# Reordering the scan's inserts between weight products in a Mamba-2 layer: decay product first, state product last, transposes ahead of the B-C products

## The chip, the cores and the metric

The kernel runs on one core of a Trainium2 chip. The metric is device time in microseconds, the median over runs. The engines named below are TensorE (PE, with its weight loads shown apart as PEld), VectorE (DVE), ScalarE (ACT), GpSimd (POOL) and SyncE (SP, whose queue issues most of the DMAs).

## The reference

One layer of a Mamba-2 mixer with a residual and two RMS norms, on 512 tokens of 2048 channels, in float32. Cut to what matters:

```python
hn = rmsnorm(x, ln_g)
proj = hn @ w_in                              # 2048 -> z 4096, x 4096, B 8*128, C 8*128, dt 64
xbc = silu(causal_depthwise_conv(xbc))        # 4 taps
dt = softplus(dt + dt_bias); a = -exp(a_log)
# scan over chunks, 64 heads of 64 channels, 8 groups of 8 heads that share B and C (128 states)
cs = cumsum(dt * a)
y_diag = einsum(C B^T, exp(cs_l - cs_s) masked to s <= l, x * dt)
y_off  = einsum(C, state, exp(cs))
state  = state * exp(cs_last) + einsum(B, exp(cs_last - cs), x * dt)
y = (y_diag + y_off + D * x) * silu(z)
out = rmsnorm(x + rmsnorm(y) @ w_out)
```

## The kernel before

The 512 tokens stand in the free dimension, channels in the partitions. The input projection is cut into 80 tiles of 128 channels. Each float32 weight tile is loaded, cast by ACT to a high part (`hi`, line 87) and its remainder is taken by DVE (`lo`, line 88); a product is then three matmuls (`hi` by `xh`, `hi` by `xl`, `lo` by `xh`).

A head pair is a "unit": 32 units `u`, four to a group `g`. A unit needs an x tile and a z tile, a group a B and a C tile. The first eight tiles (B0 C0 x0 z0 x1 z1 B1 C1) are multiplied plainly, 16 steps each. From step 128 on, the other tiles go two by two through `pair(n, prev)`, which multiplies a two by two block of weights with seven products (R11, T1, T2, R22, R21, T3, T4) over sums and differences of blocks instead of eight. A pair is 28 steps long, a step is two `k` of a product, so six matmuls; the seventh product of a pair (`last`) runs inside the next pair. There are 36 pairs, 32 of x and z, with a pair of B and C ahead of the third unit of each group. Then comes the output projection, from step 1136, with products of the same two kinds.

Between the weight products stand the small matmuls of the scan, called inserts here. They are put at steps: `add(step, f, *a)` appends a function to the list `ev[step]`, and `run(step)`, which the product loops call at the start of each step, calls that list in the order in which it was filled. So two inserts at one step run in the order of their `add` calls. The inserts of a unit are:

- `u_load` issues three DMAs on SP's queue: `csb` (the cumulated decay of two heads, spread over the partitions, one buffer) and `ecs`, in two parts.
- `u_decay` makes the decay matrix `m` (one buffer): 12 small ACT instructions, one large ACT exponential, and one DVE product with `cbm`.
- `u_xt` transposes `xs` by four matmuls into the bank `tr` (line 473); DVE makes `xd` and `xw` from it (lines 476 and 479).
- `u_state` makes the state product of `Bt` and `xw` in the bank `yo` (line 488), which ACT and DVE split into `stsh` and `stsl` (lines 403 and 404, in an `urgent` block).
- `u_yd` is the product of `xd` and `m` in the bank `yd` (lines 502 and 506), in two halves of 64 columns of the array; DVE then makes `y` from it (line 509).
- `u_yo` multiplies `Cs` and the split state (lines 518 to 520); DVE ends `y` from it (lines 521 to 523) and SP stores it (line 524).

For units 2 to 31 their steps count from the unit's own pair: 28, 42, 56, 65, 65 and 71, so `u_state` and `u_yd` share a step. Units 0 and 1 have steps of their own (`ramp`), where those two lie apart. The inserts of a group are `g_bt` (two transposes of B, for 6 of the groups at the step where unit 4g-2 has `u_state` and `u_yd`) and `g_cb` (the products of B and C in the banks `yd` and `yo`, lines 433 and 434, then `cbm`; for groups 1 to 7 at the step where unit 4g-1 has `u_xt` and unit 4g has `u_load`). Weight loads, splits and sums of a pair (`q_events`) are added after all of these, so at a shared step they follow the inserts.

TensorE, SP and GpSimd run in program order (`MANUAL`). DVE and ACT are ordered by a planner, which walks through the instructions with modelled times; instructions in an `urgent` block have priority.

Of the kernel before, what the change touches and what calls it, by code (L numbers as in the profile page):

```python
# [27 lines left out]
NU = G * UPG  # L28
# [6 lines left out]
def mamba_layer(ctx: ExitStack, tc: tile.TileContext, d: dict, out: bass.AP):  # L35
# [83 lines left out]
    at = {s: i * KT for i, s in enumerate(plain)}  # L119
# [584 lines left out]
    def add(step, f, *a):  # L704
        ev.setdefault(step, []).append((f, a))

    for g in range(1, G):
        add(at["B", g] + (30 if ("B", g) in plain else 93), g_bt, g)
        for i in range(2):
            add(at["x", 4 * g] + 28, g_cb, g, i)  # L710
    ramp = [[66, 71, 63, 75, 87, 92], [56, 65, 50, 68, 86, 92]]
    for u in range(NU):
        w = ramp[u] if u < len(ramp) else [28, 42, 56, 65, 65, 71]
        for o, f in zip(w, (u_load, u_decay, u_xt, u_state, u_yd, u_yo)):
            add(at["x", u] + o, f, u)
    for n in range(len(quads)):
        q_events(n, NPL * KT + n * QS, n == len(quads) - 1, 0 if n else 14, lone=not n)
    for i in range(4):
# [393 lines left out]
```

## Time and profile before

| what | value |
|---|---|
| median of 3 runs | 1294.51 us (1292.67 to 1301.33) |
| the profiled execution's own time | 1295.7 us |
| its span, first to last instruction | 1294.0 us |
| mean granted TensorE clock | 0.991 |
| PE busy, share of the span | 97% |
| DVE busy | 84% |
| ACT busy | 64% |
| DMA, mean rate | 175 GB/s |

The profile tells of one execution. A timeline row has the start, the time from it to the end of the row's last instruction, engine, line, what is written from what, the shape, how many instructions were merged, and in brackets the idle time before it and what ended that. A row of the waits has the engine and tile that waited, whom it waited for, the total in us, how often, and the longest. Matmuls are pipelined: a row of one matmul says 0.28, but the next starts some 0.11 us after it, so costs on TensorE are read from start to start.

### The profile page before, as it was taken

Reading aid. Unit: us, or ns where it says so; the run is one execution under the profiler, and the core shown is the slowest. Engines: PE = TensorE matmul, PEld = TensorE weight load, DVE = VectorE, ACT = ScalarE, POOL = GpSimd, SP = SyncE. Lnnn points to the kernel's source line nnn. Section 1 sums busy time; section 2 is a strip of 40 time slices with the busy share of each in tenths; the row PEclk is TensorE's granted clock in tenths of the full one; section 3 lists DMA queues with packets and bytes.
Section 4 is the critical chain, followed back from the end, with each engine's and each line's share of the span. In section 5 each row is a group of like instructions: output and inputs, shape, how many; then the busy total and the mean of one; then the engine's idle time right before and its main releaser. Section 6 shows DMA issues by size and latency. Waiting matters only on the chain.

```text
span 1294.0 us, 24519 instructions
## 1 busy us (share of the span) xinstructions
PE 1252.1 (97%) x9932; PEld 1192.9 (92%) x9932; DVE 1084.3 (84%) x1449; ACT 826.6 (64%) x1357; POOL 77.5 (6%) x99
## 2 busy tenths in 40 slices
PE   8989899999999999999999999999999899999997
PEld 8989899999999999999999999999988899899885
DVE  5796988988989898998889899889857877887865
ACT  7667667677666757767685867778666445434433
POOL 0000001010000101010100001000000000000000
PEclk9989999999999999999999999999999999999999
DMA  9546657585676667667667677766637576647612
GB/s 356 179 141 172 162 161 174 143 215 142 192 197 174 159 169 183 164 176 199 162 161 195 151 188 171 212 155 154 185 105 258 146 199 199 197 119 229 183 57 98
DMA packets 70194, 225.90 MB, mean 175 GB/s; under 512 B 8384, under 2 KB 12800, under 8 KB 69952
## 3 DMA queue, kind: packets, MB, share of 16 engines
q1 hardware_dynamic: 56688, 176.34, 40.2%
q0 software_dynamic: 12672, 46.14, 22.1%
q8 instruction: 78, 1.28, 0.4%
q10 hardware_dynamic: 720, 1.84, 0.4%
q14 instruction: 36, 0.29, 0.1%
HBM read 211.52 MB, written 12.78 MB: 173 GB/s over the span
## 4 chain that ended last, share of the span: by engine, by line
PE 74%; DVE 11%; DMA 7%; issue 4%; ACT 3%; SPq 0%; POOL 0%; DVEq 0%; ACTq 0%; POOLq 0%
PE S L637 7%; PE S L635 7%; PE S L636 7%; PE mm L635 5%; PE mm L636 4%; PE R L635 4%; PE mm L637 4%; PE R L636 4%; PE R L637 4%; DVE lo L88 3%; PE mm L929 3%; PE mm L931 3%; PE mm L930 3%; PE yd L502 2%; PE mm L867 2%
## 5 line engine op out<-in xcount | busy, mean ns | idle before, releaser
L87 ACT CAST hi<-ra 128x1024 fp32r<-128x1024 f32 x150 | 154.7, 1046 | 159.5 <-DVE ra L604 72.9
L88 DVE TENSOR_TENSOR lo<-ra,hi 128x1024 fp32r<-128x1024 f32 x150 | 181.3, 1221 | 24.2 <-ACT hi L87 24.1
L635 PE MATMUL mm<-xh,hi 128*128 128x256 f32 x576 | 163.6, 284 | 0.0
L637 PE MATMUL mm<-xh,lo 128*128 128x256 f32 x576 | 160.6, 279 | 0.6 <-DVE lo L88 0.6
L636 PE MATMUL mm<-xl,hi 128*128 128x256 f32 x576 | 160.4, 278 | 0.0
L637 PE MATMUL R<-s,lo 128*128 128x256 f32 x576 | 160.3, 278 | 0.1
L635 PE MATMUL R<-s,hi 128*128 128x256 f32 x576 | 160.2, 278 | 0.0
L636 PE MATMUL R<-s,hi 128*128 128x256 f32 x576 | 160.2, 278 | 0.0
L88 DVE TENSOR_TENSOR lo<-rc,hi 128x1024 fp32r<-128x1024 f32 x94 | 114.9, 1223 | 28.5 <-ACT hi L87 28.1
L87 ACT CAST hi<-rc 128x1024 fp32r<-128x1024 f32 x94 | 98.4, 1047 | 50.8 <-issue 29.1
L604 DVE TENSOR_TENSOR ra<-ra,rc 128x1024 f32<-128x1024 f32 x88 | 107.7, 1224 | 13.3 <-DMA rc<-in_wi 11.8
L635 PEld LDWEIGHTS mm<-xh,hi 128*128 128x128 f32 x576 | 108.1, 188 | 5.2 <-issue 5.0
L637 PEld LDWEIGHTS mm<-xh,lo 128*128 128x128 f32 x576 | 109.2, 190 | 0.8 <-DVE lo L88 0.8
L637 PEld LDWEIGHTS R<-s,lo 128*128 128x128 f32 x576 | 109.1, 189 | 0.3 <-DVE lo L88 0.3
L635 PEld LDWEIGHTS R<-s,hi 128*128 128x128 f32 x576 | 108.2, 188 | 0.0
L636 PEld LDWEIGHTS mm<-xl,hi 128*128 128x128 f32 x576 | 108.2, 188 | 0.0
L636 PEld LDWEIGHTS R<-s,hi 128*128 128x128 f32 x576 | 108.1, 188 | 0.0
L637 PE MATMUL S<-xh,lo 128*128 128x256 f32 x288 | 83.5, 290 | 5.6 <-DVE lo L88 5.6
L635 PE MATMUL S<-xh,h1h 128*128 128x256 f32 x288 | 83.4, 290 | 1.0 <-DVE xr L398 1.0
L635 PE MATMUL S<-xh,hi 128*128 128x256 f32 x288 | 81.3, 282 | 2.2 <-ACT xh L577 1.3
L636 PE MATMUL S<-xl,hi 128*128 128x256 f32 x288 | 81.2, 282 | 0.7 <-DVE xl L578 0.7
L636 PE MATMUL S<-xl,h1h 128*128 128x256 f32 x288 | 80.8, 280 | 0.0
(452 smaller groups left out, 3940.8 us busy)
## 6 DMA issues: line engine op xcount, KB each, us to landing
rc<-in_wi SPq DMA_DIRECT2D x76, 512.0 KB, 5.9
ra<-in_wi SPq DMA_DIRECT2D x42, 512.0 KB, 6.2
rb<-in_wi SPq DMA_DIRECT2D x40, 512.0 KB, 6.9
ra<-in_wi POOLq DMA_DIRECT2D x36, 512.0 KB, 6.3
rb<-in_wi POOLq DMA_DIRECT2D x36, 512.0 KB, 5.9
csb<-cscr SPq DMA_DIRECT2D x32, 512.0 KB, 8.0
ra<-in_wo SPq DMA_DIRECT2D x26, 512.0 KB, 5.4
yscr<-xs SPq DMA_DIRECT2D x32, 256.0 KB, 2.6
```

The source lines that it names most:

```text
L87: S.copy(out=hi, in_=raw)
L88: V.tensor_tensor(out=lo, in0=raw, in1=hi, op=ALU.subtract)
L502: T.matmul(pyd[r, i, :], x[:, 2 * i, hh, :], m[:, i, hh::4, :], start=i == 0, stop=False, skip_group_check=True)
L604: V.tensor_tensor(out=raw, in0=raw, in1=qs[n][other], op=ALU.add)
L635: T.matmul(ps, hi[:, k, :], ah, start=first and k == 0, stop=False, skip_group_check=True)
L636: T.matmul(ps, hi[:, k, :], al, start=False, stop=False, skip_group_check=True)
L637: T.matmul(ps, lo[:, k, :], ah, start=False, stop=k == KH - 1, skip_group_check=True)
L867: T.matmul(ps[:, t, :], yh[:, k, tt], hi[:, k, :], start=st, stop=False, skip_group_check=True)
L929: T.matmul(ps, yh, hi, start=first and k == 0, stop=False)
L930: T.matmul(ps, yh, lo, start=False, stop=False)
L931: T.matmul(ps, yl, hi, start=False, stop=last and k == 1)
```

## The change

The six functions of a unit are no longer added unit by unit behind all of the group's. They are added in four rounds: load, decay and xt of all units; then yd of all; then the group's `g_bt` and `g_cb`; then state and yo. The steps themselves stay. So at a shared step the order changes:

- at 30 steps (units 2 to 31): `u_state`, `u_yd` becomes `u_yd`, `u_state`; at 6 of them `g_bt`, `u_state`, `u_yd` becomes `u_yd`, `g_bt`, `u_state`;
- at 7 steps: `g_cb` twice, `u_xt`, `u_load` becomes `u_xt`, `u_load`, `g_cb` twice;
- at step 156: `u_yo` of unit 1, `u_load` of unit 2 becomes `u_load`, `u_yo`.

No instruction is added or removed.

```diff
+    ramp = [[66, 71, 63, 75, 87, 92], [56, 65, 50, 68, 86, 92]]
+    steps = [ramp[u] if u < len(ramp) else [28, 42, 56, 65, 65, 71] for u in range(NU)]
+
+    def add_units(*kinds):
+        for u in range(NU):
+            for i, f in kinds:
+                add(at["x", u] + steps[u][i], f, u)
+
+    add_units((0, u_load), (1, u_decay), (2, u_xt))
+    add_units((4, u_yd))
     for g in range(1, G):
         add(at["B", g] + (30 if ("B", g) in plain else 93), g_bt, g)
         for i in range(2):
             add(at["x", 4 * g] + 28, g_cb, g, i)
-    ramp = [[66, 71, 63, 75, 87, 92], [56, 65, 50, 68, 86, 92]]
-    for u in range(NU):
-        w = ramp[u] if u < len(ramp) else [28, 42, 56, 65, 65, 71]
-        for o, f in zip(w, (u_load, u_decay, u_xt, u_state, u_yd, u_yo)):
-            add(at["x", u] + o, f, u)
+    add_units((3, u_state), (5, u_yo))
```

## The prediction

> **What bounds the kernel now.** I read the page first, then busy time by stage, then TensorE's waits.
>
> ```profile
> PE 1252.1 (97%) x9932; PEld 1192.9 (92%) x9932; DVE 1084.3 (84%) x1449; ACT 826.6 (64%) x1357; POOL 77.5 (6%) x99
> ```
> ```profile
> 170.00:970.00 800.00, 794.64 (x6752) 768.50 (x6751) 705.03 (x907) 568.10 (x974) 57.53 (x67) 1.00 0.66 171
> 970.00:1294.00 324.00, 304.60 (x1985) 276.40 (x1983) 247.88 (x342) 143.02 (x197) 13.73 (x16) 0.99 0.56 169
> ```
> The second fence is the table by stage: start and end in us, length, then busy us of PE, PEld, DVE, ACT and POOL. The reader is to see that TensorE is the bound of the stage where the changed inserts lie (170 to 970 us): it is busy 794.6 of 800 us, so 5.4 us of idle time is all that better order could win there by ending waits. DVE is second with 705 of 800, and has some 95 us of air; ACT has 232. The rest of TensorE's idle time (19.4 of 324 us) lies in the output projection, which the change does not touch.
>
> Which waits those are, for 60 to 1000 us:
> ```profile
> PE S L637 <- DVE lo L88: 5.6, 9, 1.5
> ...
> PE tr L473 <- DVE win L366: 0.6, 1, 0.6
> ```
> The list has ten rows, and of the operations that the change moves only one is in it: a transpose (L473), once, in the ramp. No row has L488 (state), L502 or L506 (decay product), or L433 and L434 (B-C). So **no insert that changes places waits for anything today**; the waits of the stage are of weight products for a split (L637 for `lo`), which stand elsewhere in the pair. An order that lets an insert wait less cannot win on TensorE. What is left is the cost of changing from one kind of matmul to another, and what DVE and ACT do with other arrival times.
>
> **The change on TensorE: state and decay product.** The timeline at unit 11, today's order, with two rows of its `u_yo`:
> ```profile
> 422.54 0.28 PE L635 MATMUL mm<-xh,hi 128*128 128x256 f32 x1
> ...
> 422.77 0.28 PE L637 MATMUL mm<-xh,lo 128*128 128x256 f32 x1
> 422.88 0.60 PE L488 MATMUL yo<-xw,bt 128*128 128x128 f32 x4
> 423.42 0.65 PE L502 MATMUL yd<-m,xd 128*64 128x256 f32 x4
> ...
> 424.55 0.39 PE L506 MATMUL yd<-m,xd 128*64 128x128 f32 x4
> 424.87 0.39 PE L635 MATMUL mm<-xh,hi 128*128 128x256 f32 x1
> 425.09 0.28 PE L636 MATMUL mm<-xl,hi 128*128 128x256 f32 x1
> ...
> 429.08 0.28 PE L518 MATMUL yo<-csth,stsh 128*128 128x256 f32 x1
> ...
> 429.31 0.28 PE L520 MATMUL yo<-csth,stsl 128*128 128x256 f32 x1
> ```
> Products follow each other by (422.77 - 422.54) / 2 = 0.115 us. From 422.77 to 425.09 are 2.32 us with two products in them, so the two inserts cost 2.32 - 0.23 = **2.09 us**. The dear places are the change to the 64-column form and the way back: the state's four matmuls take 0.54 instead of about 0.44, the step out of the decay product is 0.21 (424.55 to 424.87 less a pair's 0.11), and the second product behind it comes after 0.22 instead of 0.115.
>
> The new order needs three transitions that this row doesn't have: product to decay product, decay product to state, state to product. The ramp has the first and the last, because units 0 and 1 run the two apart:
> ```profile
> 103.46 0.61 PE L488 MATMUL yo<-xw,bt 128*128 128x128 f32 x4
> 103.82 0.48 PE L198 MATMUL mm<-xh,hi 128*128 128x256 f32 x2
> 104.14 0.40 PE L198 MATMUL mm<-xl,hi 128*128 128x256 f32 x2
> 104.38 0.40 PE L198 MATMUL mm<-xh,lo 128*128 128x256 f32 x2
> ```
> ```profile
> 112.48 0.39 PE L198 MATMUL S<-xh,lo 128*128 128x256 f32 x2
> 112.80 0.65 PE L502 MATMUL yd<-m,xd 128*64 128x256 f32 x4
> ...
> 114.25 0.50 PE L198 MATMUL S<-xh,hi 128*128 128x256 f32 x2
> 114.59 0.40 PE L198 MATMUL S<-xl,hi 128*128 128x256 f32 x2
> ```
> Two products take 0.24 here. The state product alone: 104.14 - 103.46 = 0.68, less 0.24, is 0.44. The decay product alone: 114.59 - 112.80 = 1.79, less 0.24, is 1.55, and its entry is 0.32 instead of 0.24, so 1.63. Together 2.07, against 2.09 in one insert: **the costs add up, and no neighbour makes either cheaper**. Only decay product to state is not shown. Leaving the decay product costs a product 0.21 and then 0.105 of a late second start. Upper bound: the state pays both and the first products behind it pay the same again (0.2 more, by the nearest row, 424.55), 32 x 0.2 = +6.4 us. Lower bound: the state hides the second part, 32 x -0.105 = -3.4 us. (I count 32 for 30 units.) I take 0, since a state matmul and a product are both 128*128 forms and both show a start-to-start time of 0.11 behind their own kind.
>
> The late second start is 0.105 us long. The Trainium skill, "TensorE: Matmul & The Clock Gate", section "LDWEIGHTS (loading the stationary operand)", gives a weight load as its columns divided by 1.2 ns, an estimate of 107 ns for 128 columns whatever the rows. By that rule the load that nothing covers would be paid by whichever 128-column form comes next, state as well as product, so the sum would be 0 and not -3.4; the trace agrees in the size.
>
> The six steps with `g_bt` between them go the same way: two transposes move from ahead of a state product to the same place behind the decay product.
>
> **The change on TensorE: transposes and B-C products.**
> ```profile
> 415.00 0.59 PE L433 MATMUL yd<-bc 128*128 128x256 f32 x2
> ...
> 416.31 0.60 PE L473 MATMUL tr<-ident,xs 128*128 128x128 f32 x4
> ...
> 416.87 0.28 PE L636 MATMUL S<-xl,h1h 128*128 128x256 f32 x1
> ```
> ```profile
> 349.74 0.60 PE L473 MATMUL tr<-ident,xs 128*128 128x128 f32 x4
> ...
> 350.30 0.28 PE L636 MATMUL S<-xl,h1h 128*128 128x256 f32 x1
> ```
> From the first transpose to the second product are 0.56 us behind B-C products as well as behind plain ones (the second fence, where a transpose stands alone). The last B-C matmul is a 128*128 form of 128 columns like the transposes, so I give it their exit: 0 for 7 steps, with 0.1 either way at the most (0.7 us). `u_xt` now starts 1.31 us earlier and the B-C products 0.445 later. `xd` comes early and nobody waits for it; `cbm` has until `u_decay`, 14 steps of six 0.115 us matmuls, 9.7 us, later.
>
> **What DVE and ACT see.** In the new order the decay product ends 0.44 us earlier and the state 1.63 us later than today.
> ```profile
> 423.55 0.27 ACT L403 CAST stsh<-yo 128x128 fp32r<-128x128 f32 x1
> 424.99 0.40 ACT L456 ACTIVATE m<-csb,cs 128x128 f32<-128x128 f32 x1 [1.17 <-PE yd L506]
> ...
> 431.14 1.05 ACT L459 ACTIVATE m<-m 128x1024 f32<-128x1024 f32 x1
> ```
> ```profile
> 424.56 0.28 DVE L404 TENSOR_TENSOR stsl<-yo,stsh 128x128 fp32r<-128x128 f32 x1
> 424.99 0.75 DVE L509 SCALAR_TENSOR_TENSOR xs<-xs,par,yd 128x512 f32<-128x512 f32 x1
> 427.24 0.69 DVE L398 TENSOR_TENSOR xr<-mm,rbc 128x512 f32<-128x512 f32 x1 [1.50 <-PE mm L637]
> ```
> ACT waits 1.17 us for the decay product to end before it overwrites `m`. If ACT keeps `stsh` first, that cast starts at 423.55 + 1.63 = 425.18 and `m` at 425.45, 0.46 later than today; if `m` goes first, it starts at 424.55. DVE's `stsl`, if it stays ahead of `y`, goes from 424.56 to about 425.45 and `y` ends at 425.73 + 0.75 = 426.48, still ahead of 427.24, where DVE waits 1.50 us for a weight product anyway. The state is wanted at 429.08 (`stsh`) and 429.31 (`stsl`): 3.6 us remain. How often the two covers exist, from 170 to 970 us:
> ```profile
> DVE xr L398 <- PE mm L637: 33.0, 22, 1.6
> ```
> ```profile
> ACT m L456 <- PE yd L506: 24.5, 21, 1.2
> ```
> So the 0.9 us that DVE may lose lies under an existing wait in 22 of 30 units. A gain of up to 0.44 x 21 = 9 us of ACT's waiting goes into ACT's own idle time. I put both at 0 on TensorE.
>
> **The one queue order that changes: step 156.**
> ```profile
> 136.15 0.33 SPq L81 DMA_DIRECT2D rb<-in_wi  x1
> 149.02 0.33 SPq L524 DMA_DIRECT2D yscr<-xs  x1
> 149.39 0.43 SPq L440 DMA_DIRECT2D csb<-cscr  x1
> ```
> and TensorE's waits from 160 to 170 us:
> ```profile
> PE S L635 <- ACT hi L87: 0.9, 1, 0.9
> PE S L637 <- DVE lo L88: 0.8, 1, 0.8
> ```
> SP holds the loads of unit 2 (`csb`, two of `ecs`) behind the store of unit 1's `y`, which waits for DVE until 149.02. Put first, they can go at about 136.5, 12.9 us sooner. The store then stands behind three issues (the row of `csb` has 0.43 for one), long before its data. Unit 2's decay on ACT can so move ahead, out of the way of the casts that TensorE waits for soon after (the second fence). I take those 1.7 us as won; the loads may instead slow the `rb` transfer ahead of them, 0 to 1 us.
>
> **Sum**: 0 (state and decay product) + 0 (transposes and B-C) + 0 (DVE and ACT) - 1.7 (step 156) = -1.7 us on the profiled execution's own 1295.7 us, 1294.0. That execution is 1.2 us above the median of 1294.51, from which the sum gives 1292.8; I say **1293 us**. Within 1% (13 us) counts as no change for this kernel, whose own runs lie 8.7 us apart.
>
> **Rivals.**
>
> 1. *The waits for splits go* (faster). The planner has 0.44 us more room on ACT per unit, and all of `lo`'s 5.6 us go, with the 3.4 us of a hidden weight load: 1294.5 - 5.6 - 3.4 = 1285.5. For it: they are waits for just the two engines whose order the change touches. Against: they are 9 in all, the longest 1.5, so most pairs have none to lose, and the splits waited for stand elsewhere in the pair than the inserts. Chance 0.10, and hardly ever over 1%.
>
> 2. *The state's cast queues behind the decay on ACT* (slower). The decay product now ends first, so the planner may let the 12 small and one large `m` instructions go ahead of `stsh`. They ran, with what ACT does between them, from 424.99 to 431.14 + 1.05 = 432.19, 7.2 us; from 424.55 they would end at 431.75, `stsh` and `stsl` at 432.30. TensorE wants `stsl` at 429.31, so it would stand 3.0 us, in 21 units 63 us: 1357. It decides from 3.6 us of queue on. Against: the cast is `urgent` and is ready 0.6 us after `m`. Chance 0.04. The Trainium skill (the page named above, section "Architectural detail: the array is 16× 32×32, not 1× 128×128") calls ScalarE's and VectorE's queues strict first in, first out, and by that nothing behind a stuck cast could pass it; the trace agrees, in that ACT stood idle for 1.17 us for `m`.
>
> 3. *DVE's wait for the state without cover* (slower). In the 8 to 10 units without the 1.5 us wait, 0.9 us each pass to `lo` and to TensorE: up to 9 us, 1303; with the drain's +6.4 it is 1309. Chance 0.08, of which 0.04 over 1%.
>
> 4. *Nothing happens at all*: also the planner's order stays, and step 156 wins nothing: 1294.5. This is within the forecast's own range, 1290 to 1297.
>
> **Chances and range.** Forecast with rival 4: 0.78; rivals 1 to 3 as given. Faster by over 1%: 0.03; within: 0.89; slower: 0.08. The range runs from rival 1's 1286 to the drain's bound, 1294.5 + 6.4 = 1301.
>
> **What would show it.** Right: L502 ahead of L488 in TensorE's timeline, the two together 2.1 us from start to start; no row of L488, L502 or L518 to L520 among TensorE's waits; `csb`'s load at 137 us instead of 149; TensorE idle some 5 us from 170 to 970. Wrong: a wait of L520 or L518 for `stsl` or `stsh`, `m` rows ahead of `stsh` on ACT, or an insert of 1.98 or 2.3 us. The planner makes it most uncertain: it may reorder DVE anywhere, and a `lo` late by 1 us in each pair would be 30 us.

## The result and the profile after

The change makes the kernel **slower by 1.2%**: 1309.85 us (1307.74 to 1315.3, 4 runs) against 1294.24 us; the ratio is 1.0116, 95% interval 1.0068 to 1.0165. The profiled execution has a span of 1306.0 us, 12.0 above the one before. 1293 us was forecast, 1301 was the upper end.

The page's first row and the table by stage (start and end, length, busy us of PE, PEld, DVE, ACT, POOL) of the changed kernel:

```profile
PE 1249.6 (96%) x9932; PEld 1184.9 (91%) x9932; DVE 1085.0 (83%) x1449; ACT 826.3 (63%) x1357; POOL 77.8 (6%) x99
```
```profile
170.00:970.00 800.00, 780.64 (x6673) 751.25 (x6672) 700.31 (x898) 560.25 (x964) 56.93 (x66) 1.00 0.65 170
```

From 170 to 970 us TensorE now stands idle for 19.4 us instead of 5.4. Its waits from 170 to 980 us say for what:

```profile
PE S L637 <- DVE lo L88: 14.3, 15, 1.8
PE R L637 <- DVE lo L88: 2.6, 5, 0.8
```

Before, from 170 to 1000 us, there was one row for `lo` of the input projection:

```profile
PE S L637 <- DVE lo L88: 4.8, 8, 1.5
```

These are the weight products' splits again (`lo`), 20 waits instead of 8. Still no insert is in the list. So the time went where the prediction had put the waits, but it did not see what would lengthen them.

Idle time is not all of it. From the last matmul of unit 2's `u_yo` to that of unit 29's pass 745.7 us instead of 736.9, and the times from each matmul's start to the next divide the 8.8 us. At their usual pace weight products follow each other by 0.1134 us. What the steps of over 0.13 us take beyond that, in waits above all, grew by 15.7 us. What the other steps take beyond it fell by 7.0 us (there is a second, slower pace, to which the experiments come back). The steps into, within and out of the inserts sum to 92.7 us instead of 92.6. Units 30 and 31 add 4.0 us, the output projection 4.4; the stretch ahead of unit 2's `u_yo` is 5.0 us shorter. These are figures of one execution each: over all 14 profiles of this case the stretch behind unit 31 varies by 9 us, so its 4.4 us can't be put down to the change.

The chain behind the longer waits is read backwards, wait by wait. First DVE's waits from 170 to 970 us, before and after, then ACT's:

```profile
DVE ra L604 <- DMA rc<-in_wi: 11.8, 12, 2.0
```
```profile
DVE ra L604 <- DMA rc<-in_wi: 26.0, 23, 2.1
```
```profile
ACT hi L87 <- DVE ra L604: 62.1, 21, 3.8
```
```profile
ACT hi L87 <- DVE ra L604: 88.7, 25, 5.2
```

The sum of two weight pieces (L604) waits 26.0 us for the `rc` piece to land, where it waited 11.8; ACT's cast waits for that sum, and the split for the cast. Why does `rc` land later? SP's timeline about unit 12, before and then after:

```profile
455.37 0.33 SPq L524 DMA_DIRECT2D yscr<-xs  x1
455.80 0.38 SPq L81 DMA_DIRECT2D rc<-in_wi  x1
```
```profile
454.81 0.33 SPq L524 DMA_DIRECT2D yscr<-xs  x1
455.24 0.38 SPq L81 DMA_DIRECT2D rc<-in_wi  x1
```

The load of `rc` goes out right behind the store of `y`, and SP stands until that `y` is there (from 170 to 970 us, in the kernel before):

```profile
SPq L524 <- DVE xs L523: 527.6, 30, 19.0
```

Two thirds of the stage SP waits for `y`, and what stands behind it in the queue, up to four weight loads and the `csb` load, can't go out. (After the change the row has 536.7 us, hardly more: not the length of this wait makes the loss, but which load is late by it.) The last matmul of `u_yo`, from which `y` follows, dates the store:

```profile
451.84 0.28 PE L520 MATMUL yo<-csth,stsl 128*128 128x256 f32 x1
```
```profile
449.16 0.28 PE L520 MATMUL yo<-csth,stsl 128*128 128x256 f32 x1
```

Before, the store is issued 455.37 - 451.84 = 3.53 us behind it; after, 454.81 - 449.16 = 5.65. Taken so for units 2 to 29, the median goes from 3.62 to 5.41. DVE's timeline shows what came between, first before, then after:

```profile
454.00 0.75 DVE L391 SCALAR_TENSOR_TENSOR xs<-xr,par,xs 128x512 f32<-128x512 f32 x1
454.66 0.69 DVE L523 TENSOR_TENSOR xs<-xs,z 128x512 f32<-128x512 f32 x1
455.26 1.75 DVE L461 TENSOR_TENSOR m<-m,cbm 128x1536 f32<-128x1536 f32 x1
```
```profile
451.43 0.75 DVE L391 SCALAR_TENSOR_TENSOR xs<-xr,par,xs 128x512 f32<-128x512 f32 x1
452.09 1.75 DVE L461 TENSOR_TENSOR m<-m,cbm 128x1536 f32<-128x1536 f32 x1
453.76 0.42 DVE L679 TENSOR_TENSOR xr<-R,sn 128x256 f32<-128x256 f32 x1
454.10 0.68 DVE L523 TENSOR_TENSOR xs<-xs,z 128x512 f32<-128x512 f32 x1
```

**The mask product `m` of the next unit (L461, 1.75 us) has overtaken `y`'s last product (L523).** In the instruction order it stands ahead of it in 22 of 30 units; before, in none. (The eight others are units 30 and 31 and the six behind which a pair of B and C comes: of the 36 pairs, 30 are of x and z and 6 of B and C.) With the decay product first, the bank and `m` come free earlier, ACT's decay is scheduled earlier, and for the planner `m` is then ready when DVE comes to choose; by program order it is the earlier instruction. That reason is argued from the order that came out, since the planner's own times are not in a trace; that the overtaking costs the time is what the experiments test.

### The profile page after: what moved, and what is told of

The parts are those of the page before. It is cut to its first block, busy times and chain, and to the rows that moved or that the text cites. A ratio compares the mean times of both kernels' runs of the same rounds, so it can differ in the third digit from the quotient of the medians.

```text
span 1306.0 us, 24504 instructions
## 1 busy us (share of the span) xinstructions
PE 1249.6 (96%) x9932; PEld 1184.9 (91%) x9932; DVE 1085.0 (83%) x1449; ACT 826.3 (63%) x1357; POOL 77.8 (6%) x99
## 4 chain that ended last, share of the span: by engine, by line
PE 54%; DVE 20%; DMA 13%; issue 7%; ACT 5%; SPq 1%; POOL 0%; DVEq 0%; ACTq 0%; POOLq 0%
DVE lo L88 5%; PE S L637 5%; DMA csb<-cscr 4%; PE S L635 4%; PE S L636 4%; PE mm L935 3%; PE mm L937 3%; PE mm L936 3%; PE R L637 3%; PE R L636 3%; PE R L635 3%; PE mm L635 2%; PE mm L636 2%; PE mm L637 2%; DVE xs L391 2%
## 5 line engine op out<-in xcount | busy, mean ns | idle before, releaser
L604 DVE TENSOR_TENSOR ra<-ra,rc 128x1024 f32<-128x1024 f32 x88 | 107.7, 1224 | 27.5 <-DMA rc<-in_wi 26.0
```

The costliest lines, as they stand in the source:

```text
L604: V.tensor_tensor(out=raw, in0=raw, in1=qs[n][other], op=ALU.add)
```

## The experiments

Each is compared with the kernel before on the same chip, as a ratio with its 95% interval; 1.0 is the kernel before. Line numbers shift by a few where an edit adds lines.

**Which part of the change.** Only the swap:

```diff
-    add_units((0, u_load), (1, u_decay), (2, u_xt))
     add_units((4, u_yd))
     ...
-    add_units((3, u_state), (5, u_yo))
+    for u in range(NU):
+        for i, f in ((0, u_load), (1, u_decay), (2, u_xt), (3, u_state), (5, u_yo)):
+            add(at["x", u] + steps[u][i], f, u)
```

> Only the decay product is put ahead of the state product (and of the B transposes); transposes, B-C products and the step 156 stay as in the kernel before. Theory A (the decay runs earlier on ACT, so the planner puts DVE's mask product m, 1.75 us, ahead of the last product of y; the store of y, which holds SP's queue, goes 1.8 us later, and the weight loads behind it with it): all of the loss, without what step 156 wins: 1308 to 1314, TensorE idle 15 to 20 us from 170 to 970 us. Theory B (DVE and ACT stand at the head of their queues for the later state product): the same time. Theory C (the transposes ahead of the B-C products do it): as the kernel before, 1292 to 1297.

1306.42 us, 1.0098 (1.0072 to 1.0123), a little under both windows that said slower; TensorE idle 17.4 us in the stage (800 less the first number behind the length). The loss belongs to the swap, theory C is out.

```profile
170.00:970.00 800.00, 782.64 (x6660) 754.78 (x6658) 699.15 (x896) 558.93 (x963) 56.94 (x66) 1.00 0.66 170
```

Everything but the swap:

```diff
     add_units((0, u_load), (1, u_decay), (2, u_xt))
-    add_units((4, u_yd))
     ...
-    add_units((3, u_state), (5, u_yo))
+    add_units((3, u_state), (4, u_yd), (5, u_yo))
```

> The transposes go ahead of the B-C products and unit 2's loads ahead of unit 1's store, but the state product stays ahead of the decay product. Theories A and B: the loss goes and what step 156 wins stays: 1288 to 1292. Theory C: 1306 to 1312.

1292.24 us, 0.9973 (0.9952 to 0.9994): a gain of 3.5 us by the ratio. The loss is gone, as theories A and B had it, if 0.24 us above their window.

**Is it the overtaking, or the wait for the state?** The changed kernel, `y` with priority:

```diff
+        with urgent():
             V.tensor_tensor(out=ecs, in0=pyo, in1=ecs, op=ALU.mult)
             ...
             V.tensor_tensor(out=y, in0=y, in1=z, op=ALU.mult)
```

> The changed kernel, with y's last three DVE instructions given priority, so that m no longer stands ahead of them; TensorE's order and the waits for the state stay. Theory A: store of y 3.5 us behind u_yo again, TensorE idle about 5 us from 170 to 970, time 1287 to 1294. Theory B: the waits are all still there: 1304 to 1311.

1290.62 us, 0.9966 (0.9948 to 0.9984): the whole loss is gone. `m` overtakes nowhere, the store is 3.63 us behind `u_yo` again. The waits for the state are all there, 18 now instead of the 8 of the changed kernel (the two rows), so theory B falls:

```profile
DVE stsl L404 <- ACT stsh L403: 3.1, 8, 0.5
```
```profile
DVE stsl L404 <- ACT stsh L403: 4.9, 18, 0.5
```

Of its own windows one missed: 9.6 us of TensorE idle in the stage, not 5. (The profile is of the slowest of its ten executions, 1295.87 us.)

The reverse, in the kernel before:

```diff
+        with tc.issue_after(un[u + 1]["mi"].ins) if 2 <= u < 30 and u % 4 != 1 else ExitStack():
             V.tensor_tensor(out=y, in0=y, in1=z, op=ALU.mult)
```

(`mi` is the mask product `m`.)

> The kernel before with TensorE's old order, in which y's last product is made to queue behind m on DVE in 21 units. Theory A: the store goes about 2 us later and the loss appears without the change: 1303 to 1312. Theory B: no wait for the state is added: 1293 to 1297.

1304.24 us, 1.0077 (1.0042 to 1.0112). One order on DVE, with TensorE's order untouched, brings the greater part of the loss (0.8% of 1.2%, and not to be told from the 1.0% of the swap alone), with its mark, the wait for `rc`:

```profile
DVE ra L605 <- DMA rc<-in_wi: 26.0, 22, 3.0
```

A third way, without priority:

```diff
-        V.tensor_tensor(out=m6, ...)            # in u_decay
+    def u_mask(u):                              # the same product by cbm
+    for u in range(NU):
+        add(at["x", u] + steps[u][1] + 2, u_mask, u)
```

> The changed kernel, with the mask product m moved behind u_yo in program order, so that the planner puts it behind y's last product without any priority. By the planner's order as the cause: as the run with y's priority, 1288 to 1294. If that run won by its priority and not by the order: 1298 to 1309.

1289.51 us, 0.9953 (0.993 to 0.9977): the order is what counts, not the priority. With DVE's order put right in either way, the change wins 0.3 to 0.5%, not to be told from the 0.3% of the run without the swap. So the swap, apart from its effect on DVE's order, shows no cost.

**Is the path SP's queue, or DVE itself?** The changed kernel, with the overtaking left in (22 units), the stores later:

```diff
+    def u_store(u):
+        nc.sync.dma_start(yscr[u // UPG][:, u % UPG, :], un[u]["y"])
     def u_yo(u):
-        nc.sync.dma_start(yscr[u // UPG][:, u % UPG, :], y)
+        if u < 2 or u > 29:
+            u_store(u)
...
+    for u in range(2, 30):
+        add(at["x", u] + 84, u_store, u)
```

> The changed kernel, with the stores of y (units 2 to 29) issued 13 steps later, behind the next two weight loads and the next csb load in SP's queue; DVE's order keeps m ahead of y's last product in 22 units. If the loss goes through SP's queue: DVE's wait for rc from 170 to 970 us falls from 26 to about 11 or less, 1286 to 1294. If it is DVE's own order (m ahead makes the splits late): 1303 to 1310.

1281.69 us, **0.9882** (0.9851 to 0.9912), better than either window. (In the order that resulted the store stands behind four weight loads, not two, and `csb`.) DVE waits for `rc` nowhere from 170 to 970 us, and TensorE is idle 2.95 us there:

```profile
170.00:970.00 800.00, 797.05 (x6797) 768.18 (x6796) 709.58 (x920) 575.47 (x986) 57.66 (x67) 1.00 0.66 176
```

So the overtaking costs nothing where those loads don't queue behind the store. SP still stands for long, now for weight buffers that the splits have to free, and that costs nothing:

```profile
SPq L81 <- DVE lo L88: 576.0, 90, 12.8
```

How far the store has to move was then tried with 73 and 79 in place of 84, behind one load and behind four:

> The changed kernel with the stores of y 2 steps later: behind one load only, the first rc, which DVE's sum (ra plus rc) reads. If this load is the one that was late: DVE's wait for rc is gone, 1281 to 1288. If the whole row of loads is late with it: 1292 to 1305.

1283.3 us, 0.9922 (0.9896 to 0.9949). One `rc` load taken out from behind the store is nearly all of it, and DVE's wait for it is gone.

> The changed kernel with the stores of y 8 steps later: behind the four weight loads, but ahead of the csb load. If it is the weight loads that were late: 1280 to 1285. If the csb load counts as well (ACT's decay waits for it): 1285 to 1292.

1281.34 us, 0.9899 (0.9872 to 0.9926): not to be told from the run with `csb` moved too.

**What the swap is worth when SP's queue is out of the way.** The later stores without the change, and with both remedies:

> The kernel before, with the same later stores. If SP's queue is a limit there too (it stands 528 us for y, and DVE waits 11.8 us for rc), TensorE's 5.4 us of idle from 170 to 970 shrink: 1287 to 1293. If its waits have another cause: 1293 to 1297.

1289.54 us, 0.995 (0.9928 to 0.9973).

```profile
170.00:970.00 800.00, 799.16 (x6758) 772.96 (x6758) 705.33 (x912) 570.84 (x981) 56.80 (x66) 1.00 0.66 175
```

> The changed kernel with y's priority and the later stores together. If both act through SP's queue: no more than the better of the two alone, 1286 to 1292. If they are independent: 1282 to 1287.

1283.14 us, 0.9894 (0.9867 to 0.992): no more than the later stores alone (0.9882). The time itself fell into the window of the other theory, since the later stores alone had done better than expected; but that the two remedies don't add up says that both act on the same thing. With the stores out of the way, the order of `m` and `y` makes no difference that these runs can tell.

With the later stores the changed order wins 0.7% over the old one (0.9882 against 0.995, intervals apart), and that although TensorE is idle *more* (2.95 us against 0.84). (The profile of the old order with later stores is of its fastest execution, 1283.28 us, so the two profiled spans lie only 1.8 us apart; from unit 2's `u_yo` to unit 29's it takes 733.7 us, the new order 728.8.) The timelines show a second difference. It is there without the later stores too: the kernel before, then the changed one, from the second product behind unit 12's inserts to the eighteenth after it:

```profile
447.48 0.28 PE L636 MATMUL mm<-xl,hi 128*128 128x256 f32 x1
...
449.60 0.28 PE L636 MATMUL S<-s,hi 128*128 128x256 f32 x1
```
```profile
444.96 0.28 PE L636 MATMUL mm<-xl,hi 128*128 128x256 f32 x1
...
447.01 0.28 PE L636 MATMUL S<-s,hi 128*128 128x256 f32 x1
```

2.12 / 18 = 0.118 us each behind a decay product, 2.05 / 18 = 0.114 behind a state product. A busy share cannot show this. Taken over all steps of product to product from unit 2's `u_yo` to unit 29's, 47% ran at 0.117 to 0.130 us in the kernel before (2565 of 5463), 17% in the changed one (947 of 5463). Between the two runs with later stores, the same division as above gives 9.2 us for the pace, less 4.1 us for the steps of over 0.13 us: it accounts for the 5.0 us. To see whether the swap does it:

> The later stores (behind four weight loads and the csb load), with the decay product ahead of the state product, but transposes, B-C products and step 156 as in the kernel before. Theory P (weight products behind a state product run at 0.113 us each, behind a decay product often at 0.118): as the changed kernel with later stores, 1280 to 1285, under a quarter of the products at 0.117 or more. Theory X (the later stores with the change were ahead of those without by the transposes or by step 156): 1287 to 1292.

1284.43 us, 0.9922 (0.9905 to 0.9939), 20% at the slow step.

> The later stores, with the state product still ahead of the decay product, but the transposes ahead of the B-C products and the loads of unit 2 ahead at step 156. Theory P: 1286 to 1291, a third or more of the products at 0.117 or more. Theory X: 1280 to 1285.

1287.64 us, 0.9946 (0.9926 to 0.9966), 33% at it, just under the third that theory P asked for. Both times lie in theory P's windows, but the two intervals overlap, and in the two profiles (this one of the fastest execution again) the stretch from unit 2 to unit 29 differs by 1.2 us only, 729.6 against 728.4: the direction is P's, the size is not settled. The old order with later stores, without the transposes moved, has 54% (2947 of 5463), so the share depends on more than the swap. Over all 14 profiles it is 14 to 31% in the nine kernels with the swap and 33 to 54% in the five without: apart, but hardly, and one execution each. That the swap does it is not shown.

## Why the prediction was wrong

- **The bound, and that no insert waits**: right, before and after.
- **State and decay product on TensorE, 0**: right for the inserts. The new order, decay product first:

```profile
442.63 0.28 PE L637 MATMUL mm<-xh,lo 128*128 128x256 f32 x1
442.84 0.65 PE L502 MATMUL yd<-m,xd 128*64 128x256 f32 x4
...
443.97 0.39 PE L506 MATMUL yd<-m,xd 128*64 128x128 f32 x4
444.29 0.71 PE L488 MATMUL yo<-xw,bt 128*128 128x128 f32 x4
444.76 0.37 PE L635 MATMUL mm<-xh,hi 128*128 128x256 f32 x1
```

  From 442.63 to the product at 444.96 are 2.33 us, less two products of 0.114, so 2.10 against 2.09. The state pays the exit from the 64-column form (443.97 to 444.29, the same 0.32), and takes 0.47 instead of the ramp's 0.36 up to the next product: the late second start of 0.105, which the prediction had left open between the two. The Trainium skill ("TensorE: Matmul & The Clock Gate", section "LDWEIGHTS (loading the stationary operand)") gives a weight load by its columns, an estimate of 0.107 us for 128 columns; the trace agrees in the size, but that the late start is an uncovered load is not shown, and the profile's own row of such a load says 0.19 us. Over units 2 to 29 the steps at inserts sum to 92.7 us instead of 92.6, so the 0 for transposes and B-C products was right too. What the sum left out is the pace of the products behind the insert: it priced the insert and its two neighbours only. That term, 7.0 us in the two profiles, was in the change's favour.
- **What DVE and ACT see, 0**: this is the step that failed. It followed `stsl`, `y`'s first instruction and the next normalisation, found cover for each, and booked ACT's 0.44 us as harmless, because ACT has idle time. But an instruction that becomes ready earlier also takes a place earlier. What lay behind the place taken was not asked: L523, the store, and on SP's queue the loads. The runs showed, in place of the 0: `m` ahead of `y`'s last product in 22 units, the store 1.8 us later, DVE's wait for `rc` up from 11.8 to 26.0 us, TensorE idle for 19.4 us instead of 5.4; and with DVE's order alone put right, 0.9966 instead of 1.0116, so the term was worth 1.5%. The prediction's closing sentence named the danger, with 30 us for a `lo` late in each pair, but gave it no place in the sum or among the rivals. The rest of the sum came close: 1293 us is 0.999 of the kernel before, and with DVE's order put right the change stands at 0.9966 and 0.9953.
- **Step 156, -1.7**: the load moved as forecast, and the two waits between 160 and 170 us are gone:

```profile
135.45 0.43 SPq L440 DMA_DIRECT2D csb<-cscr  x1
```

  The run with transposes and step 156 alone wins 3.5 us; how it divides between the two was not tried, so the 1.7 us are not shown.
- **Rival 2** (the cast behind the decay): did not come with its price, though its sign did: in 21 of 30 units the planner put the cast behind two small instructions of `m`, and TensorE waited for no state. **Rival 3** was the nearest, DVE late and `lo` with it, but by another way than a wait for the state. Its 0.9 us per unit was measured as 3.1 us over eight waits.
- **The range** left the case out: 0.08 on slower was low for a change that lets a planner choose again, and 1301 had no term for a new order on DVE.

## What to carry to other kernels

When a change makes something ready earlier on an engine that a planner orders, ask what it will be put ahead of, and follow that instruction to the DMA that waits for it and to what queues behind the DMA. A store that waits for late data does not belong in front of loads: look in the waits of the issuing queue for the engine that it stands for longest, here 528 of 800 us, and see whether a load behind it is late; if so, move the store behind that load. The length of the wait does not tell by itself: with the later stores SP stood 576 us for weight buffers, and TensorE was idle for 2.95 us. Moving the store behind one load turned this change from a loss of 1.2% into a gain of 0.8%. The fastest versions measured, 1281.3 and 1281.7 us, are the changed order with its stores moved.

## What was not expected of the hardware

The Trainium skill says ("DMA: Bandwidth & Descriptors", section "Issuing engines are not separate DMA queues") that DMAs from several engines share the same DMA engines, and that spreading them saves only the time to initiate them. No run here changed which engine issues a DMA; but the order within one issuing queue was worth 0.5% with the old order of inserts and 2.3% with the new one (0.9882 / 1.0116), since SP issues nothing behind a DMA that waits for its data (the 527.6 us row, and the `rc` load 0.43 us behind the store in both timelines).

Weight products of one form run at two paces, 0.114 and 0.118 us from start to start, for dozens of matmuls in a row, with a granted clock shown as 1.00 in both. What sets the pace was not found. The insert's last matmul alone does not: of the steps behind a decay product (up to the next insert or wait) 34 to 54% ran at the slow pace and behind a state product 3 to 29%, but behind `u_yo`, whose matmuls are the same in every kernel, the share lies between 7 and 71%.
